# The first product of a squared-ReLU MLP as seven block products, with first and second product by turns

## The chip, the cores and the metric

The kernel runs on one core of a Trainium2 chip. The metric is device time in microseconds (us) of one execution. The kernel before the change takes 1112.21 us (median of three runs, 1112.17 to 1113.17).

Names used below: PE is the matrix engine (its weight loads have a queue of their own in the profile, PEld), DVE the vector engine, ACT the scalar engine, POOL the general-purpose engine, SP the engine that here only issues DMAs. Each engine works through its own list of instructions in the order of that list; an instruction that waits for a semaphore holds back everything behind it on the same engine. DMAs are issued from SP (plain loads), from POOL (loads that add into their destination) and, in a few places, from ACT.

## What is computed

A two-layer decoder trunk of 512 tokens with 1024 features: a gated linear attention layer, then a stick-breaking attention layer, each followed by a layer norm, an MLP and another layer norm. The change touches the MLP of both layers:

```python
def sq_relu_mlp(x, w_up, w_down):
    h = jax.nn.relu(x @ w_up)
    return (h * h) @ w_down

for layer in range(DEPTH):            # DEPTH = 2
    ...                               # mix = gla_mixer(...) or attention
    h = layer_norm(DEEPNORM_ALPHA * h + mix, ln_g[layer, 0], ln_b[layer, 0])
    h = layer_norm(DEEPNORM_ALPHA * h + sq_relu_mlp(h, mlp_w_up[layer], mlp_w_down[layer]),
                   ln_g[layer, 1], ln_b[layer, 1])
```

x is 512 x 1024, w_up 1024 x 4096, w_down 4096 x 1024, all float32.

## The kernel before

**Three products for one.** Each float32 operand is split in two reduced-precision parts, hi and lo, and a product is hi·hi + hi·lo + lo·hi: three PE instructions for each 128x128 block of the stationary operand (`mm3`, L91 to L95, or the same three written out). A weight tile of 128x1024 elements is split by `split_tile` (L66): an ACT copy makes hi (L70), a DVE subtraction makes lo (L72). hi and lo tiles come from two rings of six buffers each, raw tiles from one of three (L60). `put` (L97 to L99) does the same for activations, into tiles called T (`unit`).

**Seven for eight.** `seven` (L300) computes a product of 1024 inner elements as a 2x2 by 2x2 block product with seven block products in place of eight, at the price of sums and differences of blocks. Its moving operand is a weight block of 512 columns, its stationary operand 128 tokens of activations. Of the eight weight tiles B of a call, two blocks come as sums made by the DMA (a plain load on SP, L320, then an accumulating load on POOL onto the same tile, L314) and two more sums are made by DVE from tiles in place (L379, L389), or, with `ends`, by further accumulating loads. Each block product is 24 PE instructions of 512 columns (L355) for each of two row tiles of 128 tokens; DVE adds each result from PSUM to the residual rows h (`Rows.add`, L167 and L169).

**The MLP** (`mlp`, L694) works on groups of 512 of the 4096 inner features, eight a layer. `up(g)` computes one group of the first product directly: 8 blocks of the inner dimension x 4 blocks of features x 3 parts, 96 PE instructions with 512 tokens as moving columns (the group g = 0 in two passes of 256 tokens each, since the second half of the tokens is normalised last); then ReLU (ACT, L719) and the square (DVE L721 or ACT L723). `down(g)` is one call of `seven` on two groups. The order is up(0), up(1), up(2), down(0), up(3), up(4), down(2), and so on: between the `down` calls stand two `up` calls, which use raw tiles and no tile B.

**Around it.** `finish` (L245) follows the last product before the MLP: as row tiles of 128 tokens become complete, `stats` (a DVE reduction, two small POOL instructions L183 and L184) and `centre` (L190) normalise them, and `turn_affine` (L226) transposes them on PE, applies scale and shift on ACT (L234) and splits them into T tiles. The turns of the third and fourth row tile are handed to the MLP (`late`) and stand between the matmuls of its first group. After up(1), DVE applies the layer norm's scale and shift to the rows h themselves (`affine`, L196).

**What sets the order.** The instructions are written in program order; a scheduler then places them on the engines by readiness and priority, except those marked `keep_in_program_order`. The lists that it leaves are fixed; the chip follows them.

## Time and profile before

| | |
|---|---|
| median of the runs | 1112.21 us |
| profiled execution, its own time | 1111.48 us |
| span of the profiled execution | 1109.5 us |
| ACT busy | 571.8 us (52%) |
| POOL busy | 145.7 us (13%) |
| DMA | 169.06 MB, 152 GB/s over the span |

The span is what the profiler records between the first and the last instruction; the profiled execution's own time is 2.0 us longer. Busy time of an engine is the time in which at least one of its instructions ran. PE instructions overlap one another in the records (each is shown longer than the distance to the next), so a busy share near 100% on PE means that it never stood still for long, and its pace is read from the distance of starts.

### The profile page before, as it was taken

To read this page: it belongs to the slowest core of one execution; us is meant where nothing else is said; L and a number is where in the kernel's file an instruction comes from. 1 tells how busy PE (TensorE), PEld (TensorE's weight loads), DVE (VectorE), ACT (ScalarE), POOL (GpSimd) and SP (SyncE) were. 2 spreads that over 40 slices of the span, in tenths; PEclk is the share of its full clock that TensorE was granted. 3 is DMA by queue.
4 is the path that set the end of the run, shared out by engine and by line. 5 is a ranking of instruction groups with operands and counts; after the bars stand their busy time and mean duration, and the time that the engine had idled before them with its cause. 6 is when DMAs were issued, how large, how long until landed. Compare 5 with 4: busy or idle time off the path is not lost.

```text
span 1109.5 us, 14388 instructions
## 1 busy us (share of the span) xinstructions
PE 1100.6 (99%) x5503; PEld 912.1 (82%) x5503; DVE 817.8 (74%) x1029; ACT 571.8 (52%) x853; POOL 145.7 (13%) x177
## 2 busy tenths in 40 slices
PE   9999999999999999999999999999999999999997
PEld 7888888898888888888888777788988888888885
DVE  4687639957966856858898886688579667667677
ACT  4455437653533533536675666775635335336363
POOL 1011222210100100122202200211100000001132
PEclk9999999999999999999999999999999999999999
DMA  8441399493670670788847342443937806706774
GB/s 254 119 133 57 109 259 201 140 286 108 188 211 19 193 207 23 201 202 149 239 87 199 96 134 97 108 81 109 311 103 203 236 26 187 211 20 192 175 129 93
DMA packets 111352, 169.06 MB, mean 152 GB/s; under 512 B 13178, under 2 KB 38138, under 8 KB 111284
## 3 DMA queue, kind: packets, MB, share of 16 engines
q1 hardware_dynamic: 86228, 119.39, 32.8%
q0 software_dynamic: 22592, 44.04, 23.0%
q10 hardware_dynamic: 2464, 4.72, 1.2%
q8 instruction: 43, 0.70, 0.3%
q14 instruction: 25, 0.20, 0.1%
HBM read 162.89 MB, written 3.15 MB: 150 GB/s over the span
## 4 chain that ended last, share of the span: by engine, by line
PE 94%; DVE 3%; ACT 1%; issue 1%; POOL 0%; POOLq 0%; DVEq 0%; ACTq 0%
PE ps L355 30%; PE ps L93 18%; PE ps L94 18%; PE ps L95 18%; PE ps L796 3%; PE ps L1039 2%; PE ps L977 1%; PE ps L943 1%; PE ps L991 1%; DVE lo L72 1%; PE ps L231 1%; PE ps L584 0%; PE ps L121 0%; DVE h L167 0%; DVE c L968 0%
## 5 line engine op out<-in xcount | busy, mean ns | idle before, releaser
L355 PE MATMUL ps<-hi,T 128*128 128x512 f32 x1008 | 313.5, 390 | 0.1
L93 PE MATMUL ps<-T,hi 128*128 128x512 f32 (+1 forms) x776 | 290.4, 375 | 0.0
L94 PE MATMUL ps<-T,hi 128*128 128x512 f32 (+1 forms) x776 | 287.5, 371 | 0.5 <-DVE T L99 0.4
L95 PE MATMUL ps<-T,lo 128*128 128x512 f32 (+1 forms) x776 | 287.1, 370 | 0.0
L72 DVE TENSOR_TENSOR lo<-raw,hi 128x1024 fp32r<-128x1024 f32 x126 | 153.2, 1221 | 95.3 <-ACT hi L70 95.1
L355 PEld LDWEIGHTS ps<-hi,T 128*128 128x128 f32 x1008 | 189.0, 188 | 40.0 <-DVE T L99 0.6
L70 ACT ACTIVATE hi<-raw 128x1024 fp32r<-128x1024 f32 x128 | 135.4, 1061 | 167.4 <-PE ps L355 52.7
L70 ACT ACTIVATE hi<-B 128x1024 fp32r<-128x1024 f32 x118 | 124.4, 1059 | 173.3 <-PE ps L94 106.2
L72 DVE TENSOR_TENSOR lo<-B,hi 128x1024 fp32r<-128x1024 f32 x118 | 142.9, 1222 | 85.1 <-ACT hi L70 85.1
L355 PE MATMUL ps<-lo,T 128*128 128x512 f32 x504 | 196.3, 389 | 0.0
L95 PEld LDWEIGHTS ps<-T,lo 128*128 128x128 f32 x776 | 146.3, 189 | 24.8
L94 PEld LDWEIGHTS ps<-T,hi 128*128 128x128 f32 x776 | 146.4, 189 | 24.2 <-DVE T L99 1.0
L93 PEld LDWEIGHTS ps<-T,hi 128*128 128x128 f32 x776 | 146.1, 189 | 24.3 <-issue 1.0
L314 POOL DMA_DIRECT2D B<-in_mlp_w_down_dram x52 | 62.9, 1264 | 543.5 <-DMA B<-in_mlp_w_down_dram 342.9
L355 PEld LDWEIGHTS ps<-lo,T 128*128 128x128 f32 x504 | 94.7, 188 | 19.5
L169 DVE TENSOR_TENSOR h<-h,ps 128x512 f32<-128x512 f32 x108 | 73.4, 682 | 2.7 <-PE ps L355 2.4
L99 DVE TENSOR_TENSOR T<-s,T 128x1024 fp32r<-128x1024 f32 (+1 forms) x52 | 54.8, 1055 | 8.3 <-ACT T L98 8.3
L98 ACT ACTIVATE T<-s 128x1024 fp32r<-128x1024 f32 (+1 forms) x52 | 48.5, 937 | 21.4 <-DVE s L721 14.3
L968 DVE TENSOR_TENSOR_SCAN c<-r,c 128x384 f32<-128x384 f32 (+2 forms) x64 | 49.2, 818 | 3.3 <-ACT c L965 3.2
L93 PE MATMUL ps<-hi,T 128*128 128x512 f32 x128 | 51.4, 402 | 0.0
L719 ACT ACTIVATE s<-ps 128x512 f32<-128x512 f32 x64 | 37.8, 593 | 25.8 <-PE ps L95 25.2
L95 PE MATMUL ps<-hi,T 128*128 128x512 f32 x128 | 50.3, 393 | 0.0
(210 smaller groups left out, 1292.0 us busy)
## 6 DMA issues: line engine op xcount, KB each, us to landing
raw<-in_mlp_w_up_dram SPq DMA_DIRECT2D x64, 512.0 KB, 5.4
B<-in_mlp_w_down_dram SPq DMA_DIRECT2D x64, 512.0 KB, 5.4
B<-in_mlp_w_down_dram POOLq DMA_DIRECT2D x52, 512.0 KB, 7.8
raw<-in_gla_w_in_dram SPq DMA_DIRECT2D x20, 512.0 KB, 3.8
raw<-in_mlp_w_down_dram SPq DMA_DIRECT2D x16, 512.0 KB, 4.5
B<-in_gla_w_o_dram POOLq DMA_DIRECT2D x14, 512.0 KB, 9.0
raw<-in_kv_w_dram SPq DMA_DIRECT2D x12, 512.0 KB, 4.5
B<-in_gla_w_o_dram SPq DMA_DIRECT2D x8, 512.0 KB, 6.3
```

The costliest lines, as they stand in the source:

```text
L70: keep(nc.scalar.activation(hi, raw, AF.Copy))
L72: keep((on or nc.vector).tensor_tensor(lo, raw, hi.bitcast(F32), op=ALU.subtract))
L93: keep(nc.tensor.matmul(ps, lhsT=a[0], rhs=b[0], start=first, stop=False))
L94: keep(nc.tensor.matmul(ps, lhsT=a[0], rhs=b[1], start=False, stop=False))
L95: keep(nc.tensor.matmul(ps, lhsT=a[1], rhs=b[0], start=False, stop=last))
L98: keep(nc.scalar.activation(hi, ps, AF.Copy))
L99: keep((on or nc.vector).tensor_tensor(lo, ps, hi.bitcast(F32), op=ALU.subtract))
L169: nc.vector.tensor_tensor(h, h, ps, op=op)
L314: nc.gpsimd.dma_start(out=b.rearrange("p (a b) -> p a b", a=2), in_=weights(k, h, j), accum_op=ALU.add)
L355: nc.tensor.matmul(banks[s], lhsT=a(k, s)[x], rhs=b[k][y], start=opens and (k, x, y) == (0, 0, 0), stop=closes and (k, x, y) == (3, 1, 0), ...
L719: nc.scalar.activation(s2[:, f, :], pss[f], AF.Relu)
L968: nc.vector.tensor_tensor_scan(down, r[:, at][:, ::-1], down, 0.0, op0=ALU.mult, op1=ALU.add)
```

## The change

`up` now computes 1024 inner features a call, four calls a layer, as seven block products too. Here the weights are the stationary operand, as before (features in the rows of the result), and the moving operand is a block of 256 tokens: 7 products x 16 pairs of blocks x 3 parts = 336 PE instructions of 256 columns a call. Its seven token operands, sums and differences of blocks of x among them, are made once a layer, in the first call (c = 0), and kept (`ops`): five in T tiles, two in tiles of the hi and lo rings, which grow from six to eight buffers. Results of the block products are joined by `fresh` (ACT) and `close` (DVE additions from PSUM, then ReLU and square on ACT).

`up(c)` and `down(c)` now take turns: up(0), down(0), up(1), down(1), up(2), down(2), up(3), down(3). Both take their weight blocks from the same eight tiles B through the new class `Blocks`: (0,0) and (1,0) are loaded plainly, (0,1) and (1,1) with an accumulating load of (0,0) or (0,1) on top; `onto` then adds (1,1) onto (0,0) and (0,0) onto (1,0), by DVE or, for blocks named in `by`, by an accumulating DMA from tile to tile. The order of the loads is `AHEAD`, in up(0) its second half first. The rows' `affine` moves into up(0) and down(0). The turns of tokens 256 to 511 no longer split (class `Halves`): only x blocks (0,0) and (0,1) of tokens 0 to 255 are split at once. A few other tiles (layer-norm vectors, cumulative sums, shifted values) move into the hi and lo rings.

```diff
+            for k, j, other in order:
+                got = []
+                for h in range(2):
+                    b = pool.tile([P, 1024], F32, tag="B", bufs=8, name=nm("B"))
+                    nc.sync.dma_start(out=b.rearrange("p (a b) -> p a b", a=2), in_=weights(k, h, j))
+                    if other:
+                        nc.gpsimd.dma_start(out=b.rearrange("p (a b) -> p a b", a=2), in_=weights(other[0], h, other[1]),
+                                            accum_op=ALU.add)
...
+        def onto(self, a, b):
+            for x, y in zip(self.b[a], self.b[b]):
+                if a in self.by:
+                    nc.gpsimd.dma_start(out=x, in_=y, accum_op=ALU.add)
+                else:
+                    tt(x, x, y, op=ALU.add)
+
+    AHEAD = (0, 0, None), (1, 0, None), (0, 1, (0, 0)), (1, 1, (0, 1))
...
+        def up(c, also=()):
...
+                bs = Blocks(mlp_, w, AHEAD[2:] + AHEAD[:2], ((0, 0), (1, 0)))
...
+            product(ops[0], p1, ys, True, False, (lambda n: n == 8 and len(late) > 1 and late.pop(0)()) if c == 0 else None)
+            fresh(ys, 0, 0)
+            if c:
+                p2 = bs.pieces(1, 0)
+            product(ops[1], p2, xs, True, True, (lambda n: n == 4 and late and late.pop(0)()) if c == 0 else None)
+            close(xs, 0, 0)
+            p = bs.pieces(0, 1)
+            if c == 0:
+                r11, r21, r12, r22 = hT.r[0][:, :, LO], hT.r[0][:, :, HI], hT.r[1][:, :, LO], hT.r[1][:, :, HI]
+                t = temp()
+                tt(t, r22, r21, op=ALU.subtract)
+                ops[2] = operand(t)
+            bs.onto((0, 0), (1, 1))
+            product(ops[2], p, zs, True, False)
+            fresh(zs, 1, 1)
+            bs.onto((1, 0), (0, 0))
...
+            product(ops[3], p, ys, False, False)
+            fresh(ys, 0, 1)
...
+            product(ops[4], p, zs, False, True)
+            close(zs, 0, 1)
...
+            product(ops[5], p, ys, False, False)
+            close(ys, 1, 1)
...
+            product(ops[6], p, ys, False, True)
...
+        for c in range(NC - 1):
+            a1, a2 = up(c, turns[:2] if c == 0 else ())
+            for _ in down(c, a1, a2, by=((1, 0),), also=turns[2:] if c == 0 else ()):
                 pass
...
+        a1, a2 = up(NC - 1)
+        steps = down(NC - 1, a1, a2, norms=range(NT) if l == 0 else (2, 3), by=((0, 0), (1, 0)))
```

**The lists, at three places.** In the rows, s are the MLP's inner features, T and A split activations, B weight blocks, lo and hi their split parts, ps PSUM banks, h the residual rows; a wait on DMAHW is for a load from SP, on DMASW for a DMA from POOL.

First place: DVE at the end of an `up` and the start of the `down` behind it. Before (down(2), its first splits and the first sum of blocks among the squares of the `up` ahead):

```order
L72 TENSOR_TENSOR lo_3208<-B_3184,hi_3206 128x1024 [waits PE_49,Activation_49]
L721 TENSOR_TENSOR s_3036<-ps_2936,s_3036 128x512 [waits Activation_49]
L379 TENSOR_TENSOR B_3184<-B_3178,B_3184 128x1024 [waits DMASW2_49,DVE_49]
L721 TENSOR_TENSOR s_3036<-ps_2937,s_3036 128x512 [waits Activation_49]
L721 TENSOR_TENSOR s_3036<-ps_2938,s_3036 128x512 [waits Activation_49]
L72 TENSOR_TENSOR lo_3212<-B_3194,hi_3210 128x1024 [waits DMAHW1_49,PE_49,Activation_49]
```

Now (the end of up(2), whose fifth and sixth products are added by L830, and the first splits of down(2)):

```order
L72 TENSOR_TENSOR lo_4109<-B_4084,hi_4107 128x1024 [waits DMAHW6_49,PE_49,Activation_49]
L830 TENSOR_TENSOR s_3663<-s_3663,ps_3788 128x2x256 [waits PE_49]
L830 TENSOR_TENSOR s_3663<-s_3663,ps_3789 128x2x256 [waits PE_49]
L761 TENSOR_TENSOR B_4084<-B_4084,B_4098 128x1024 [waits DMASW4_49,DVE_49]
L72 TENSOR_TENSOR lo_4113<-B_4086,hi_4111 128x1024 [waits DMAHW7_49,Activation_49]
L761 TENSOR_TENSOR B_4086<-B_4086,B_4101 128x1024 [waits DMASW5_49,DVE_49]
L830 TENSOR_TENSOR s_3663<-s_3663,ps_3664 128x2x256 [waits PE_49]
L99 TENSOR_TENSOR T_4143<-s_3663,T_4143 128x4x256 [waits Activation_49]
L830 TENSOR_TENSOR s_3663<-s_3663,ps_3665 128x2x256 [waits PE_49]
L72 TENSOR_TENSOR lo_4148<-B_4088,hi_4146 128x1024 [waits DMAHW0_49]
```

The sum of blocks (L761) waits for the accumulating load of B_4098 and stands ahead of the second split that the first product of `down` needs (lo_4113) and ahead of the additions that close the sixth product (L830).

Second place: DVE at the end of a `down` and the start of the next `up`. Before (the last additions to the rows, then splits of raw tiles, which wait for plain loads):

```order
L167 SCALAR_TENSOR_TENSOR h_1639<-h_1639,ps_2650 128x512 [waits PE_49]
L72 TENSOR_TENSOR lo_3049<-raw_3045,hi_3047 128x1024 [waits DMAHW4_49,Activation_49]
L167 SCALAR_TENSOR_TENSOR h_1640<-h_1640,ps_2664 128x512 [waits PE_49]
L72 TENSOR_TENSOR lo_3055<-raw_3051,hi_3053 128x1024 [waits DMAHW5_49,Activation_49]
L72 TENSOR_TENSOR lo_3061<-raw_3057,hi_3059 128x1024 [waits DMAHW6_49,PE_49,Activation_49]
```

Now (the end of down(1); lo_3718 and lo_3722 are for the second product of up(2), lo_3780 and lo_3784 for its third):

```order
L72 TENSOR_TENSOR lo_3722<-B_3640,hi_3720 128x1024 [waits DMAHW7_49,Activation_49]
L761 TENSOR_TENSOR B_3634<-B_3634,B_3648 128x1024 [waits DMASW0_49,DVE_49]
L169 TENSOR_TENSOR h_1640<-h_1640,ps_3367 128x512 [waits PE_49]
L761 TENSOR_TENSOR B_3636<-B_3636,B_3651 128x1024 [waits DMASW1_49,DVE_49]
L169 TENSOR_TENSOR h_1641<-h_1641,ps_3381 128x512 [waits PE_49]
L72 TENSOR_TENSOR lo_3780<-B_3642,hi_3778 128x1024 [waits DMASW6_49,Activation_49]
```

Two sums that wait for accumulating loads have come in ahead of the splits of the third product.

Third place: POOL where the MLP of the first layer begins. Before (the statistics of the four row tiles, then accumulating loads):

```order
L184 TENSOR_TENSOR rs_1925<-ve_1924,mhalf 128x1 [waits Pool_49]
L183 TENSOR_SCALAR ve_2023<-mv_2022 128x1 [waits DVE_49]
L184 TENSOR_TENSOR rs_2024<-ve_2023,mhalf 128x1 [waits Pool_49]
L183 TENSOR_SCALAR ve_2044<-mv_2043 128x1 [waits DVE_49]
L184 TENSOR_TENSOR rs_2045<-ve_2044,mhalf 128x1 [waits Pool_49]
L314 DMA B_2614<-in_mlp_w_down_dram 128x2x512 [waits DMASW7_49,DMASW6_49,DMAHW4_49,DMASW5_49,Activation_49]
```

Now:

```order
L737 DMA B_2082<-in_mlp_w_up_dram 128x2x512 [waits DMAHW4_49,DMASW0_49]
L737 DMA B_2085<-in_mlp_w_up_dram 128x2x512 [waits DMAHW5_49]
L759 DMA B_2088<-B_2082 128x1024 [waits DMASW5_49,DMAHW6_49,DMASW0_49,Activation_49]
L759 DMA B_2090<-B_2085 128x1024 [waits DMAHW7_49,DMASW1_49]
L183 TENSOR_SCALAR ve_2020<-mv_2019 128x1 [waits DVE_49]
L184 TENSOR_TENSOR rs_2021<-ve_2020,mhalf 128x1 [waits Pool_49]
L759 DMA B_2092<-B_2088 128x1024 [waits DMAHW0_49,DMASW2_49]
L759 DMA B_2094<-B_2090 128x1024 [waits DMAHW1_49,DMASW3_49]
L183 TENSOR_SCALAR ve_2041<-mv_2040 128x1 [waits DVE_49]
L184 TENSOR_TENSOR rs_2042<-ve_2041,mhalf 128x1 [waits Pool_49]
```

The statistics of the third row tile (ve_2020) now stand behind two tile-to-tile accumulations that wait for accumulating loads, those of the fourth (ve_2041) behind two more that wait for the first two.

More of the change, by code (lines that the diff above doesn't have):

```diff
@@ L261, in finish @@
                 hs[t].centre()
-        return [lambda work, t=t: turn(t, work) for t in rest]
+        return [lambda t=t: turn(t) for t in rest]
     def rows(sp, t, pcs, ks):
@@ L741, in mlp, with temp, operand @@
-        sq.append(last)
-        steps = down(NG - 2, begun=begun, norms=range(NT) if l == 0 else (2, 3), ends=True)
-        got = done(steps, work, four, mlp_)
+            return mlp_.tile([P, 4, 512], F32, tag="s2", bufs=2, name=nm("s2"))
+        def temp():
+            return wts.tile([P, 4, 256], F32, tag="raw", bufs=3, name=nm("tmp"))
+        def operand(a, apart=False):
+            if apart:
+                us = [wts.tile([P, 2, 512], F32R, tag=tag, bufs=8, name=nm("A")) for tag in ("hi", "lo")]
+                for n, u in enumerate(us):
+                    put(u[:, :, LO], u[:, :, HI], a[:, 2 * n:2 * n + 2, :])
+            else:
+                us = [unit(F32R)]
+                put(us[0][:, :, LO], us[0][:, :, HI], a)
+            return views(us)
@@ new lines, in down, with other, add, part @@
+        def down(c, a1, a2, norms=(), by=(), also=()):
+            w = lambda k, h, j: block(mlp_w_down[l], 1024 * c + 512 * k + 256 * h, 512 * j)
+            a11, a21, a12, a22 = a1[:, :, LO], a1[:, :, HI], a2[:, :, LO], a2[:, :, HI]
+            bs = Blocks(mlp_, w, AHEAD, by)
+            ys, xs, zs = ([None, None] for _ in range(3))
+            seen = set()
+            also = list(also)
+            def other():
+                if also:
+                    also.pop(0)()
+            def add(s, banks, i, j, last=False):
+                hs[2 * i + s].add(j, banks[s], c == 0 and (i, j, s) not in seen, last and 2 * i + s in norms,
+                                  ALU.subtract if j else ALU.add)
+                seen.add((i, j, s))
+            def part(s, a, b, banks, opens, closes):
+                if opens:
+                    banks[s] = bank()
+                for k in range(4):
+                    for x, y in ((LO, 0), (LO, 1), (HI, 0)):
+                        nc.tensor.matmul(banks[s], lhsT=a(k)[:, x][:, P * s:P * s + P], rhs=b[k][y],
+                                         start=opens and (k, x, y) == (0, LO, 0),
+                                         stop=closes and (k, x) == (3, HI), skip_group_check=True)
+            def product(a, b, banks, opens, closes, i, j, last=False):
+                for s in range(2):
+                    part(s, a, b, banks, opens, closes)
+                    add(s, banks, i, j, last)
+            first = operand(a11)
+            product(first, bs.pieces(0, 0), ys, True, False, 0, 0)
+            second = operand(a12), bs.pieces(1, 0)
+            other()
+            product(*second, xs, True, True, 0, 0, last=True)
+            t = temp()
+            tt(t, a22, a21, op=ALU.subtract)
+            third = operand(t), bs.pieces(0, 1)
+            other()
+            bs.onto((0, 0), (1, 1))
+            product(*third, zs, True, False, 1, 1)
+            minus(t, t, a11)
+            bs.onto((1, 0), (0, 0))
+            fourth = operand(t), bs.pieces(0, 0)
+            product(*fourth, ys, False, False, 0, 1)
+            minus(a12, a12, t)
+            p3 = operand(a12), bs.plain(1, 1)
+            tt(a11, a11, a21, op=ALU.subtract)
+            p7 = operand(a11), bs.pieces(1, 1)
+            p4 = operand(a22), bs.pieces(1, 0)
+            for s in range(2):
+                part(s, *p3, zs, False, True)
+                add(s, zs, 0, 1, last=True)
+                yield s
+            for s in range(2):
+                part(s, *p7, ys, False, False)
+                add(s, ys, 1, 1, last=True)
+                yield ~s
+            for s in range(2):
+                part(s, *p4, ys, False, True)
+                add(s, ys, 1, 0, last=True)
+                yield 2 + s
@@ L855, in values, with done0 @@
         return held
-    def done0(steps, work, four, pool):
+    def done0(steps, four, pool):
         h2T.grow()
@@ L890, in wide @@
     def wide():
-        return [sbp.tile([P, 2 * S], F32, tag="d", bufs=2, name=nm("d")) for _ in range(2)]
+        return [wts.tile([P, 2 * S], F32, tag=tag, bufs=8, name=nm("d")) for tag in ("hi", "lo")]
     def differences(n):
```

199 lines of the change are left out of this document (134 added, 65 removed).

## The prediction

> **What bounds the kernel now.** I read the page from its head: span, busy times, slices, chain.
>
> ```profile
> span 1109.5 us, 14388 instructions
> PE 1100.6 (99%) x5503; PEld 912.1 (82%) x5503; DVE 817.8 (74%) x1029; ACT 571.8 (52%) x853; POOL 145.7 (13%) x177
> PE   9999999999999999999999999999999999999997
> DVE  4687639957966856858898886688579667667677
> PEclk9999999999999999999999999999999999999999
> DMA  8441399493670670788847342443937806706774
> PE 94%; DVE 3%; ACT 1%; issue 1%; POOL 0%; POOLq 0%; DVEq 0%; ACTq 0%
> ```
>
> PE is never idle in any slice but the last, its clock is granted in full throughout, and 94% of the chain that ended last is PE. So an instruction taken from PE is time gained, as long as the operands still come in time; and every stall of PE is time lost, since there is none now. DVE is the second engine (74%, with slices at 9), and the DMA share reaches 8 and 9 where weights are fetched. The first MLP in two stretches (an `up` with its `down`), by windows:
>
> ```profile
> core 0: us, PE busy (x) PEld busy (x) DVE busy (x) ACT busy (x) POOL busy (x), PEclk, DMA share, GB/s
> 281.80:320.00 38.20, 38.20 (x170) 31.64 (x169) 32.93 (x36) 19.48 (x20) 4.78 (x4) 1.00 0.83 224
> 320.00:363.50 43.50, 43.50 (x194) 36.03 (x193) 27.59 (x28) 15.15 (x19) 0.00 (x0) 1.00 0.23 73
> sum 81.70, PE 81.70 PEld 67.67 DVE 60.52 ACT 34.63 POOL 4.78; mean PE 40.85 PEld 33.84 DVE 30.26 ACT 17.32 POOL 2.39
> ```
>
> The first stretch is a `down`, the second two calls of `up`. PE stands at 100% in both, DVE at 86% and 63%, and DMA at 83% and 23%: the `up` calls, which need no tile B, are the time in which everything for the next `down` is fetched and summed.
>
> **The gain on PE.** The pace of PE comes from distances of starts.
>
> ```profile
> 281.97 38.08 PE ps L355 x168
> ...
> 213.40 0.28 PE L93 MATMUL ps<-T,hi 128*128 128x256 f32 x1
> ...
> 219.03 0.28 PE L95 MATMUL ps<-T,lo 128*128 128x256 f32 x1
> ```
>
> The first row, of the chain, gives 38.08/168 = 0.2267 us for 512 columns; the other two are the first and the last of 48 instructions of 256 columns (L93, L94, L95 by turns), 5.63/47 = 0.120 us. First product before, a layer: seven groups of 96 at 0.2267 and 192 half-width ones at 0.120, 152.3 + 23.0 = 175.4 us. After: 4 calls x 336 x 0.120 = 161.3 us. That is 14.1 us a layer, **28.2 us** in all. It is less than an eighth, since two of 256 columns cost 0.240 where one of 512 costs 0.227.
>
> The Trainium skill ("TensorE: Matmul & The Clock Gate", section "Wait — 56ns, not 53.3ns?") gives an instruction's time as N/2.4 GHz plus some 2.5 ns; by that, as an estimate, 512 columns take 215.8 ns and 256 take 109.2 ns, and the gain would be 38.4 us. The rows here (226.7 and 120.0) disagree.
>
> **The work added on DVE, ACT and DMA.**
>
> ```profile
> 456.97 0.68 DVE L169 TENSOR_TENSOR h<-h,ps 128x512 f32<-128x512 f32 x1
> 457.56 1.22 DVE L99 TENSOR_TENSOR T<-T,T 128x1024 fp32r<-128x1024 f32 x1
> 458.70 1.22 DVE L72 TENSOR_TENSOR lo<-raw,hi 128x1024 fp32r<-128x1024 f32 x1
> ...
> 482.79 2.00 ACT L70 ACTIVATE hi<-B 128x1024 fp32r<-128x1024 f32 x2
> ...
> L379 DVE TENSOR_TENSOR B<-B,B 128x1024 f32<-128x1024 f32 x12 | 14.6, 1216 | 0.0
> ```
>
> Behind one another, DVE starts a 512-element instruction after 0.60 us and a 1024-element one after 1.14; ACT's copies take 1.00. Seven products split 14 tiles where `up` twice split 16, but blocks used twice are split twice and the direct weights remain: 48 more splits in all (55 us), some 12 more sums of blocks (14 us), about 16 us for the operands of `up`, less 5 for squares that become fewer additions: near 80 us, DVE from 818 to about 898 us. An `up` with its `down` then asks DVE for about 63 us in 40.3 + 38.1 = 78.4 us of PE, 81% where the windows show 74%. That is no bound by itself: its cost is nothing as long as the remaining 15 us of slack a pair cover it. They don't cover a DVE that stands in front of a DMA, and that is what the lists of after show. In before, the sums of blocks never waited (L379, idle before 0.0), because the loads behind them had been out for two calls of `up`:
>
> ```profile
> 414.74 0.37 SPq L64 DMA_DIRECT2D raw<-in_mlp_w_up_dram  x1
> ...
> 441.94 12.94 SPq L320 DMA_DIRECT2D B<-in_mlp_w_down_dram  x4
> ...
> 446.03 1.20 POOL L314 DMA_DIRECT2D B<-in_mlp_w_down_dram  x1 [56.98 <-DMA B<-in_mlp_w_down_dram]
> ...
> B<-in_mlp_w_down_dram SPq DMA_DIRECT2D x64, 512.0 KB, 5.4
> B<-in_mlp_w_down_dram POOLq DMA_DIRECT2D x52, 512.0 KB, 7.8
> ...
> q1 hardware_dynamic: 86228, 119.39, 32.8%
> q0 software_dynamic: 22592, 44.04, 23.0%
> ```
>
> After, both calls use the same eight tiles B, so a load starts only when the last call has split the tile for its seventh product. SP issues one in 0.37 us. From the queues' rows a plain tile of 0.524 MB takes 0.328 x 1109.5 x 0.524/119.39 = 1.60 us of all 16 engines, an accumulated one 3.04. The page's medians from issue to landing are 5.4 and 7.8. What either takes with little beside it, and an accumulation in a crowd, by the same view over 272 to 284 us and over 388 to 396 us:
>
> ```profile
> B<-in_mlp_w_down_dram SPq DMA_DIRECT2D x1, 512.0 KB, 3.5
> B<-in_mlp_w_down_dram POOLq DMA_DIRECT2D x1, 512.0 KB, 5.9
> ...
> B<-in_mlp_w_down_dram POOLq DMA_DIRECT2D x1, 512.0 KB, 10.3
> ```
>
> I price each place with an accumulation at 5.9, 7.8 and 10.3 us, and take the middle.
>
> **From `up` to `down`** (c = 1, 2; four times). Let t be the end of the fifth product of `up`; sixth and seventh, 48 x 0.120 = 5.8 us each, end at t + 11.5. Two of eight hi buffers hold operands, so the splits of the seventh product reuse the fourth's: with ACT and DVE they are done at about t - 6.3 and t - 2.9. Then SP issues block (1,0)'s second half, (0,1) and (1,1): landings at t + 0.6 and 1.6 us apart, so B_4098's accumulation goes out at t + 5.6 and lands at t + 11.5, **13.4** or 15.9. DVE stands before L761 for it. Behind it are the sum (1.14) and lo_4113 (1.14), done at t + 15.7 in the middle case; the first product wants it at t + 13.1 (after six of its instructions): 2.6 us. B_4101 lands 1.6 us later; behind its sum stand the additions that close the sixth product, then ReLU, square and the operand a22 - a21: about 0.5 more at the second product, 2.7 at the third. Sum 4.0, **5.8**, 8.4; 23 us for four.
>
> **From `down` to `up`** (c = 2, 3; four times). With D the start of `down`, its seventh product's splits end at D + 27.0 and 28.2. SP then issues (1,0), two raw tiles, (0,1) and (1,1); the seventh of these lands at 27 + 3.5 + 6 x 1.6, so the accumulation of B_3648 goes out at D + 40.3 and lands at 46.2, 48.1 or 50.6. Two sums, two additions to the rows and the split lo_3780 end at D + 50.7, 52.7, 55.2; the third product wants it at D + 49.8: 0.9, 2.9, 5.4, and up to 4 more where the place before has made DVE late. I take **5**; 20 us for four.
>
> **Last `down` of a layer.** There `onto` for (0,0) is a tile-to-tile accumulation, which the trace doesn't show: at least nothing beyond the load before it, at most another 10.3 us. ACT's copy of the summed block stands ahead of the ReLU and square of a21 in its list. 2 to 6, **4**; twice, 8 us. The first `down` to up(1) is like the second place with earlier splits: 0 to 5, **3**; 6 us.
>
> **Where the MLP begins.** POOL's statistics now stand behind chains of accumulations.
>
> ```profile
> 216.31 0.57 POOL L184 TENSOR_TENSOR rs<-ve,mhalf 128x1 f32<-128x1 f32 x1
> ...
> 216.91 0.81 DVE L190 TENSOR_SCALAR h<-h,mv,rs 128x1024 f32<-128x1024 f32 x1 [0.65 <-POOL rs L184]
> ...
> 218.19 0.81 DVE L190 TENSOR_SCALAR h<-h,mv,rs 128x1024 f32<-128x1024 f32 x1 [0.46 <-POOL rs L184]
> ```
>
> The centring of the third and fourth row tile started 0.03 us after POOL's 0.57. Following the new list, the third's ends at 220.3 us and the fourth's, two accumulations later, starts near 227: their transposes are wanted earlier, for 4.1, **6** or 10 us in the first layer. In the second, all but the first tile's statistics may stand so: 0 to 12, **6**. Together 12.
>
> **Sum.** Stalls 23 + 20 + 8 + 6 + 12 = 69; all at their lone rows 28, all at their crowded ends 114. The profiled execution took 1111.48 us by its own time (span and 2.0 us). 1111.5 - 28.2 + 69 = 1152; I say 1150, which against the median of the runs (0.7 higher) changes nothing.
>
> **Rivals.**
> 1. *The waits are covered: faster.* If a plain load and its accumulation together take no more than about 7 us at the first place (13.1 less 2.3 of DVE leaves t + 10.8 for the landing, 5.2 us after issue), no queue stands in front of PE, and only 4 us of the starts remain: 1111.5 - 28.2 + 4 = **1087**. For it: the quickest plain load is 3.5 us. Against it: even the lone accumulation took 5.9. The Trainium skill ("DMA: Bandwidth & Descriptors", section "Anatomy of one DMA — SWDGE (gpsimd) path") gives about 2.0 us plus bytes/436e3 for such a transfer; that estimate is 3.2 us for a tile, with which this rival holds; the rows (5.9, 7.8, 10.3) disagree.
> 2. *Only the starts and the last calls pay,* the rest at lone landings: 28 us or a little less of stall, **1100 to 1112**. For it: the mean DMA rate is 152 GB/s and the windows reach 224, so a tile may land faster than the median. Against it: loads now go out in one burst, the crowded case.
> 3. *DMA or DVE is starved:* late splits make late loads, and every pair starts later than the last. All terms near their upper ends, **1175 to 1200**. For it: 81% of DVE is wanted, and SP stands in order before each tile. Against it: a stall of PE gives the others time to catch up.
>
> That the change doesn't save PE work can be left out: the count of instructions is fixed and 0.120 us was measured on the same shape.
>
> **How the numbers follow.** The forecast (1123 to 1173, centre 1150) 0.60; rival 1 0.13; rival 2 0.14, of which 0.09 faster and 0.05 the same; rival 3 0.13. Hence faster by over 0.2% 0.22, within 0.2% 0.05, slower 0.73; 0.2% is about what a measurement of this kernel can tell from no change. The range leaves out half of rival 1 and most of rival 3's upper end: 1092 to 1186.
>
> **What would show it.** Right: PE's share falls from 99% to near 93%, with idle time before the matmuls of `down` and of `up` ended by DVE's lo and T; DVE idle before L761, ended by DMA, of several us at each `up` and `down`; POOL's L183 standing behind L759; 256-column instructions of `up` 0.120 us apart. Wrong: accumulations that land within 5 us, L761 without idle time, or PE near 99% still (then rival 1). If the 256-column pitch were 0.1165 or less, a layer would cost 156.6 us or less, the gain would be 37 us or more, and the forecast would be too high by nine.

## The result, and the profile after

The changed kernel takes 1220.26 us (median of four runs, 1215.45 to 1221.53) where the kernel before takes 1112.55 in the same series: ratio 1.096, interval 1.0928 to 1.0992. The forecast was 1150 us, its range 1092 to 1186: the sign was right, the size was not. The profiled execution took 1221.53 us. One run of e1_pin_sums, below, took 2748.54 us, more than twice as long as its three others, and is left out of its median. The head of the page of after:

```profile
span 1219.8 us, 16750 instructions
PE 1113.7 (91%) x6463; PEld 963.8 (79%) x6463; DVE 895.8 (73%) x1095; ACT 672.1 (55%) x963; POOL 187.5 (15%) x217
PE   9999998599978978998899999996999979979977
PEclk9999999799998998998999899997899979989989
```

Against the page of before: PE has fallen from 99% to 91%, with slices at 5 to 8 where the MLPs lie, and in or next to the same slices the granted clock (PEclk) is no longer 9 throughout; the view of cores gives its mean as 0.949, where before it is 0.999. The busy sum of PE shows nothing of the saving (1113.7 us against 1100.6), because instructions at the lower clock last longer. So the idle time is read from the view of PE's waits in after (engine and line that wait, what for, then us in all, times, longest):

```profile
PE ps L816 <- DVE s L830: 41.6, 4, 11.0
PE ps L261 <- DVE h L190: 21.4, 5, 10.5
PE ps L909 <- ACT T L98: 15.6, 4, 6.6
PE ps L261 <- DVE mv L182: 11.5, 2, 8.1
PE ps L816 <- ACT T L98: 2.2, 2, 1.6
PE ps L816 <- DVE T L99: 2.1, 2, 1.3
```

All its rows come to 100.3 us, those of before to 3.0. So PE stands 97.3 us longer and has 28.2 us less to do: 69 us, where the span grew by 110.3. Nearly all the rest is the clock. Windows over one of the stalls (columns as in the prediction) show it:

```profile
core 0: us, PE busy (x) PEld busy (x) DVE busy (x) ACT busy (x) POOL busy (x), PEclk, DMA share, GB/s
359.00:370.00 11.00, 0.26 (x2) 0.22 (x2) 4.46 (x5) 1.01 (x1) 1.20 (x1) 0.64 0.82 153
370.00:376.00 6.00, 6.00 (x30) 6.00 (x31) 3.73 (x4) 3.02 (x3) 1.79 (x2) 0.53 0.27 53
376.00:390.00 14.00, 14.00 (x72) 11.99 (x72) 11.29 (x12) 9.43 (x12) 0.00 (x0) 1.00 0.85 238
```

PE stands for 11 us, and the granted clock falls during the stall. When PE resumes at 370, it runs the next 6 us at 0.53 and only from 376 on at full clock. In the PE timeline (start, duration, engine, line, operation) this is:

```profile
358.76 0.28 PE L816 MATMUL ps<-A,lo 128*128 128x256 f32 x1
369.78 0.80 PE L816 MATMUL ps<-T,hi 128*128 128x256 f32 x2 [10.74 <-DVE s L830]
...
375.71 0.40 PE L816 MATMUL ps<-T,hi 128*128 128x256 f32 x2
```

Between the last two rows start 27 instructions in 5.93 us; at 0.120 us each they would take 3.24. This stall costs 10.7 us of standing and 2.7 of slow running. Summed in this way over the 15 stretches of half clock in which PE had work, the slow running costs 35 to 38 us, by what is taken for the distance at full clock; PE ran for 72 us in these stretches, and half of that is 36. The whole account, place by place (stalls from the PE timeline; slow running, at its upper value, from the distances of starts in the stretch behind each; the 3.0 us of before are taken off in the row "elsewhere"):

| place | forecast | stalls | slow running behind them |
|---|---|---|---|
| `up` to `down`, four times | 23 | 41.6 | 10.1 |
| `down` to `up`, four times | 20 | 0 | 0 |
| last `down` of a layer, twice | 8 | 11.6 | 5.6 |
| first `down` of a layer | 6 | 4.0 | 3.7 |
| start of the MLP, twice | 12 | 25.0 | 10.2 |
| ahead of the first MLP, and behind it | not priced | 11.5 | 4.2 |
| elsewhere | not priced | 3.6 | 4.1 |
| sum | 69 | 97.3 | 37.9 |

Less 28.2, the two columns make 107.0 of the 110.3 us; 3.3 are not assigned (6.2 with 35 us of slow running).

**Up to down.** DVE at the end of up(1), from its timeline; the brackets hold the idle time ahead of an instruction and what ended it:

```profile
352.92 1.28 DVE L830 TENSOR_TENSOR s<-s,ps 128x512 f32<-128x512 f32 x2
365.36 1.23 DVE L761 TENSOR_TENSOR B<-B,B 128x1024 f32<-128x1024 f32 x1 [11.16 <-DMA B<-in_mlp_w_down_dram]
366.50 1.22 DVE L72 TENSOR_TENSOR lo<-B,hi 128x1024 fp32r<-128x1024 f32 x1
367.90 1.23 DVE L761 TENSOR_TENSOR B<-B,B 128x1024 f32<-128x1024 f32 x1 [0.18 <-DMA B<-in_mlp_w_down_dram]
369.04 0.68 DVE L830 TENSOR_TENSOR s<-s,ps 128x512 f32<-128x512 f32 x1
```

DVE stands 11.16 us before the sum L761 until the accumulating load has landed. Behind it stand a split, the second sum, and then the addition L830 that reads the sixth product from its PSUM bank. PE's seventh product writes to the same bank (`ys` in both calls of `product`), so PE waits for that addition, a product earlier than the forecast had it. The page's groups (busy, mean ns of one, then idle time before) and its DMA issues (median us to landing):

```profile
L761 DVE TENSOR_TENSOR B<-B,B 128x1024 f32<-128x1024 f32 x36 | 43.2, 1222 | 77.2 <-DMA B<-in_mlp_w_down_dram 44.3
...
B<-in_mlp_w_up_dram SPq DMA_DIRECT2D x64, 512.0 KB, 4.4
B<-in_mlp_w_down_dram SPq DMA_DIRECT2D x64, 512.0 KB, 4.7
B<-in_mlp_w_up_dram POOLq DMA_DIRECT2D x32, 512.0 KB, 9.3
B<-in_mlp_w_down_dram POOLq DMA_DIRECT2D x32, 512.0 KB, 9.6
B<-B POOLq DMA_DIRECT2D x28, 512.0 KB, 5.2
```

The sums, which never waited before, now wait 77.2 us in all. Plain loads got a little quicker (4.4 and 4.7 against 5.4), accumulating ones slower (9.3 and 9.6 against 7.8).

**Where the MLP begins.** From the timelines of POOL, ACT and DVE in after: the last accumulating load of the product ahead of the first MLP and the ACT copy that waits for it, then the statistics and the centring of the third row tile.

```profile
199.88 1.20 POOL L342 DMA_DIRECT2D B<-in_gla_w_o_dram  x1 [6.91 <-DMA B<-in_gla_w_o_dram]
...
207.59 1.06 ACT L70 ACTIVATE hi<-B 128x1024 fp32r<-128x1024 f32 x1 [12.44 <-DMA B<-in_gla_w_o_dram]
...
236.31 0.56 POOL L183 TENSOR_SCALAR ve<-mv 128x1 f32<-128x1 f32 x1
...
237.57 0.81 DVE L190 TENSOR_SCALAR h<-h,mv,rs 128x1024 f32<-128x1024 f32 x1 [11.78 <-POOL rs L184]
```

The lower pair was foreseen: the statistics stand behind two tile-to-tile accumulations, and DVE waits 11.78 us for them. The upper one was not: this `seven` call is not in the diff, but the scheduler has put the three chained accumulating loads of one tile behind those of the other (in before they went out by turns), and ACT waits 12.44 us for the last.

### The profile page after: what moved, and what is told of

Its sections match the earlier page's. It is cut to its first block, busy times and chain, and to the rows that moved or that the text cites. A ratio compares the mean times of both kernels' runs of the same rounds, so it can differ in the third digit from the quotient of the medians.

```text
span 1219.8 us, 16750 instructions
## 1 busy us (share of the span) xinstructions
PE 1113.7 (91%) x6463; PEld 963.8 (79%) x6463; DVE 895.8 (73%) x1095; ACT 672.1 (55%) x963; POOL 187.5 (15%) x217
## 5 line engine op out<-in xcount | busy, mean ns | idle before, releaser
L70 ACT ACTIVATE hi<-B 128x1024 fp32r<-128x1024 f32 x206 | 216.7, 1058 | 198.6 <-PE ps L909 38.9
L72 DVE TENSOR_TENSOR lo<-B,hi 128x1024 fp32r<-128x1024 f32 x206 | 247.6, 1221 | 87.8 <-ACT hi L70 87.6
L909 PE MATMUL ps<-hi,T 128*128 128x512 f32 x896 | 285.2, 398 | 15.7 <-ACT T L98 15.6
L816 PE MATMUL ps<-T,hi 128*128 128x256 f32 x1280 | 246.4, 295 | 45.8 <-DVE s L830 41.6
L816 PEld LDWEIGHTS ps<-T,hi 128*128 128x128 f32 x1280 | 211.3, 203 | 49.8 <-DVE s L830 43.4
L909 PEld LDWEIGHTS ps<-hi,T 128*128 128x128 f32 x896 | 171.4, 192 | 55.1 <-ACT T L98 17.3
L816 PE MATMUL ps<-T,lo 128*128 128x256 f32 x640 | 185.5, 293 | 0.0
L816 PEld LDWEIGHTS ps<-T,lo 128*128 128x128 f32 x640 | 129.0, 203 | 0.1
L761 DVE TENSOR_TENSOR B<-B,B 128x1024 f32<-128x1024 f32 x36 | 43.2, 1222 | 77.2 <-DMA B<-in_mlp_w_down_dram 44.3
L816 PE MATMUL ps<-A,hi 128*128 128x256 f32 x512 | 93.0, 284 | 0.8 <-ACT s L824 0.6
L816 PEld LDWEIGHTS ps<-A,hi 128*128 128x128 f32 x512 | 79.8, 192 | 1.4 <-ACT s L824 1.4
L93 PE MATMUL ps<-T,hi 128*128 128x512 f32 (+1 forms) x200 | 80.1, 401 | 0.0
L95 PE MATMUL ps<-T,lo 128*128 128x512 f32 (+1 forms) x200 | 76.6, 383 | 0.0
L94 PE MATMUL ps<-T,hi 128*128 128x512 f32 (+1 forms) x200 | 76.5, 382 | 0.0
L816 PE MATMUL ps<-A,lo 128*128 128x256 f32 x256 | 72.4, 283 | 0.0
```

The source lines that it names most:

```text
L70: keep(nc.scalar.activation(hi, raw, AF.Copy))
L72: keep((on or nc.vector).tensor_tensor(lo, raw, hi.bitcast(F32), op=ALU.subtract))
L93: keep(nc.tensor.matmul(ps, lhsT=a[0], rhs=b[0], start=first, stop=False))
L94: keep(nc.tensor.matmul(ps, lhsT=a[0], rhs=b[1], start=False, stop=False))
L95: keep(nc.tensor.matmul(ps, lhsT=a[1], rhs=b[0], start=False, stop=last))
L761: tt(x, x, y, op=ALU.add)
```

## The experiments

In each, PE's idle time is the sum of all rows of its view of waits: 100.3 us in after. The edits are to the changed kernel.

**Theory and rival for the largest place.** The theory: the sum L761, too early in DVE's list, holds up the additions, and through the PSUM bank the seventh product. The rival: PE wants the loads' blocks anyway, and if the sum stood later, PE would wait for those instead.

*e1_pin_sums.* The scheduler may no longer move `down`'s first sums ahead of what is written before them.

```diff
-        def onto(self, a, b):
+        def onto(self, a, b, keep=lambda ins: ins):
...
-                    tt(x, x, y, op=ALU.add)
+                    keep(tt(x, x, y, op=ALU.add))
...
-            bs.onto((0, 0), (1, 1))
+            bs.onto((0, 0), (1, 1), tc.keep_in_program_order)
```

The last two lines stand in `down`.

> Edit: in down, the two DVE sums of (1,1) onto (0,0) (L761) may no longer stand ahead of the splits of the third product; nothing else is pinned. Theory 1 (order): these sums, waiting for accumulating loads, held back the additions that read the sixth product's banks, which the seventh writes again. Then the four stalls before the seventh product (10.7, 11.0, 11.0, 8.8 us in the changed kernel's trace) go, and with each some 2.5 us of half clock: about 50 us less, 1170 us. Rival (the loads are late for whoever uses them): the stalls move to the fourth product of down, and no more than 15 us are gained, 1205 us or more.

Measured: 1163.54 us (median of three), ratio to before 1.0461 [1.0439, 1.0483], PE's idle time 59.7 us. The two largest rows of PE's waits in e1 were second and third in after:

```profile
PE ps L261 <- DVE h L190: 21.3, 5, 10.4
PE ps L909 <- ACT T L98: 13.7, 4, 5.9
```

The row L816 <- DVE s L830 is gone, all four stalls with it, and no other has grown by over 2 us. In e1's DVE timeline the first of these sums now starts without idle time before it, 4 us into the first product of `down` (from 367.0):

```profile
371.07 1.22 DVE L761 TENSOR_TENSOR B<-B,B 128x1024 f32<-128x1024 f32 x1
```

The gain of 56.7 us (55.1 by the spans of the profiled executions) is more than the idle time (41.6): with the slow running behind these stalls (10.1) it is 51.7, and some 4 us are not assigned. So the loads are in time, and the wait is one of order alone; the rival falls.

*e2_other_banks.* The order stays, but the seventh product gets PSUM banks of its own. It leaves out the sum of the earlier products in that quarter of the features.

```diff
-            product(ops[5], p, ys, False, False)
+            product(ops[5], p, ys, False, True)
...
-            product(ops[6], p, ys, False, True)
+            ys = [None, None]; product(ops[6], p, ys, True, True)
```

> Edit: the seventh product of up goes to two PSUM banks of its own, and the sum of the earlier products is left out of that quarter of the features; the order on DVE at the ends of the second and third up is unchanged, so the sums (L761) still stand where they stood. Theory 1a (banks): the seventh product then starts at once; DVE still stands before the sums until about t + 11.7, so what is left is what the prediction worked out for a lone landing, about 4 us at each of the four places in place of 10.4, and less half clock: 1185 to 1195 us. Rival (the seventh product waits for something else that is late at the same moment): no change, 1215 to 1221 us.

Measured: 1213.51 us, 1.0893 [1.0868, 1.0919], idle 93.4 us: a miss. Rows of PE's waits in e2:

```profile
PE ps L909 <- ACT T L98: 25.9, 8, 7.3
...
PE ps L909 <- DVE h L169: 10.0, 4, 3.4
PE ps L909 <- DVE lo L72: 9.2, 8, 2.0
```

The wait at L816 is gone as the theory says, but `down` then waits for the split behind the sum (9.2), for the additions to the rows h, which DVE reaches late (10.0), and for an operand (25.9 against 15.6). Together that is 29.5 us, 7.4 a place in place of 10.4. It bears on the forecast: even with its premise (the first waiter is `down`'s first product) the place would have cost more than the 5.8 us it gave, since it followed the two splits and left out the backlog behind them.

*e3_keep_warm.* The stalls stay, but PE runs 85 products whose results nothing reads during each of the four. It tells the clock from the idle time.

```diff
+            if c in (1, 2):
+                spare = bank()
+                for n in range(85):
+                    tc.keep_in_program_order(nc.tensor.matmul(spare[:, 0:256], lhsT=ops[5](0)[:, 0:P], rhs=ops[5](0)[:, LO],
+                                                              start=True, stop=True, skip_group_check=True))
             product(ops[6], p, ys, False, True)
```

> Edit: between the sixth and the seventh product of the second and third up, 85 matmuls of 256 columns into a spare bank, which nobody reads, 85 x 0.12 = 10.2 us at full clock, about the length of the four stalls. All other lists stay as they are. If the half clock behind each stall comes from PE standing still, no half-clock stretch is left at these four places, each gives back about 2.5 us, less up to 1.4 us where the stall was shorter: about 8 us less than the changed kernel, 1212 us. Rival (the clock falls for another reason, such as load on the chip): the half-clock stretches stay and the time is the same or longer, 1220 us or more.

Measured: 1214.87 us, 1.0946 [1.0913, 1.0980], mean clock 0.972. The windows of e3 over the same stall:

```profile
359.00:370.00 11.00, 11.00 (x94) 11.00 (x93) 2.36 (x2) 2.49 (x3) 2.31 (x2) 1.00 1.03 204
370.00:376.00 6.00, 4.68 (x37) 4.27 (x36) 5.82 (x6) 2.12 (x2) 0.66 (x1) 1.00 0.01 4
```

DVE comes to the additions no earlier (the sum waits 11.19 us in e3), yet the clock stays at 1.00 on both sides, here and at the other three places. So the half clock is a consequence of standing. The execution is 5.4 us shorter by medians (7.1 by the spans of the profiled executions), although PE did more, but the two intervals overlap: that the half clock costs time is read from the distances of starts above, not from this difference.

**Where the MLP begins.** *e4_stats_first* holds the tile-to-tile accumulations of up(0), and the last accumulating load, back until POOL's statistics have been issued (`tc.issue_after`; the list `rss` collects the last instruction of each row tile's statistics, in a line not shown).

```diff
...
+                        with tc.issue_after(rss[-3]) if order[0][2] and k and h else ExitStack():
+                            nc.gpsimd.dma_start(out=b.rearrange("p (a b) -> p a b", a=2), in_=weights(other[0], h, other[1]),
+                                                accum_op=ALU.add)
...
+                    with tc.issue_after(rss[-1]) if self.first else ExitStack():
+                        nc.gpsimd.dma_start(out=x, in_=y, accum_op=ALU.add)
```

> Edit: on POOL, in the first up of each layer, the tile-to-tile sums are issued behind the statistics of the fourth row tile, and the last accumulating load behind those of the second; order only. If POOL's queue is what held the rows' centring, the stalls of 10.5 us in the first layer and 8.1 and 2.2 us in the second go, with some 2.5 us of half clock each: 20 to 27 us less, 1193 to 1200 us. Rival (the sums themselves are then late for the fourth product): the stall moves there, and less than 8 us are gained.

Measured: 1207.80 us, 1.0867 [1.0844, 1.0890]; a gain of 12.5 where 20 to 27 were expected. The row L261 <- DVE h has shrunk from 21.4 to 1.1 us, but one product later PE has a new one (in e4 the line L816 has become L820):

```profile
PE ps L820 <- ACT T L100: 17.4, 2, 10.6
```

ACT's copy of the block that the accumulation sums stands ahead, in ACT's list, of the operand that PE wants. In the profiled execution, the quickest of four, the stall ahead of the first MLP was 3.0 us in place of 8.1, which this edit does not aim at; part of the 12.5 us may be that. *e5_act_behind* adds to e4 that this copy keeps its place behind.

```diff
-            p = bs.pieces(0, 0)
+            p = bs.pieces(0, 0, tc.keep_in_program_order) if c == 0 else bs.pieces(0, 0)
```

> Edit: the one before (statistics first on POOL), and in the first up of each layer the copies and subtractions that split the summed block (0,0) may no longer stand ahead of what is written before them on ACT and DVE. In the run before, the stalls of the first up (10.4 us in the first layer, 8.1 us in the second) came back one product later (10.6 and 6.8 us), behind an ACT copy that waited for a tile-to-tile sum. Theory (queue order on ACT): with the copies behind, both go but for the lateness of the sums themselves, 2 to 3 us in the first layer; with the half clock some 18 us less than the run before, 1188 to 1194 us. Rival (the sums are too late for the fourth product itself): the stalls move there, and less than 6 us are gained.

Measured: 1200.59 us, 1.0796 [1.0779, 1.0814]: 7.2 us less than e4, where some 18 were expected. PE's waits in e5:

```profile
PE ps L913 <- ACT T L100: 20.8, 4, 6.0
...
PE ps L820 <- ACT T L100: 7.0, 2, 6.4
```

The 10.6 us of the first layer have become 1.5; the second layer's 6.4 stay, where ACT waits for a plain load, and the stalls of the first `down` have grown from 2.1 and 1.9 to 4.9 and 4.6. Ahead of the first MLP the stall is 9.2 us, so the profiled executions of e4 and e5 differ by 6.2 us at a place that the edit does not touch. Twice, then, a wait that was taken away came back in part further down.

**The last down, and the product ahead of the MLP.** *e6_last_down* lets DVE make the sum that the last `down` made by tile-to-tile accumulation, and keeps it behind the splits of the third product; *e7_chains_by_turns* lets the two tiles of `seven` ahead of the MLP take turns in their chains of accumulating loads.

```diff
-            bs.onto((0, 0), (1, 1))
+            bs.onto((0, 0), (1, 1), tc.keep_in_program_order if c == NC - 1 else lambda ins: ins)
...
-        steps = down(NC - 1, a1, a2, norms=range(NT) if l == 0 else (2, 3), by=((0, 0), (1, 0)))
+        steps = down(NC - 1, a1, a2, norms=range(NT) if l == 0 else (2, 3), by=((1, 0),))
```

```diff
...
-        for h, (b22, b12, b11, b21) in enumerate(bs):
-            if ends:
-                for k, j in ((0, 0), (0, 1), (1, 1)):
-                    more(b21, h, k, j)
-            else:
-                tt(b21, b21, b11, op=ALU.add)
+        for k, j in ((0, 0), (0, 1), (1, 1)):
+            for h, (b22, b12, b11, b21) in enumerate(bs):
+                tc.keep_in_program_order(more(b21, h, k, j))
```

> Edit, on the changed kernel: in the last down of each layer the sum onto (0,0) is made by DVE, behind the splits of the third product, in place of a tile-to-tile accumulation. Theory (ACT's copy of the summed block stands ahead of the ReLU and square of a21 and waits for that accumulation): the stalls of 5.0 and 6.6 us go, with 2.3 and 3.3 us of half clock, 17 us less: 1200 to 1208 us. Rival (a21 is late for another reason): no change.

> Edit, on the changed kernel: in the product ahead of the first MLP, which the change does not touch, the two chains of three accumulating loads onto the halves of block (1,0) are issued by turns again, as they stood before the change; POOL's list alone differs. Theory (the new list put one chain behind the other): the stall of 8.1 us ahead of the first row tile's transposes goes, with 1.8 us of half clock: 10 us less, 1210 us. Rival (the other loads of the new first up crowd these out): no gain, 1216 us or more.

Measured: e6 1201.59 us, 1.0812 [1.0765, 1.0860], the stalls of 5.0 and 6.6 now 1.9 and 1.1; e7 1206.38 us, 1.0837 [1.0807, 1.0867], the stall of 8.1 gone. Both near what was expected: e7 gained 13.9 us for 10, and e6 gained 18.7 us, where 8.6 of stall and 5.6 of slow running make 14.2; its interval is some 10 us wide, so the difference says nothing.

**All together.** *e8_all_orders* holds the edits of e1, e4, e5, e6 and e7. It tells whether idle time and clock are the whole of the loss: the floor is then 1083 us, the time before less 28.2.

> All order edits together: sums behind the splits of the third product in every down, the last one too; statistics first on POOL; the first up's split of the summed block in written order; the chains ahead of the first MLP by turns. If the stalls are independent, 55 + 12 + 18 + 17 + 10 us are gained on 1220: 1108 us; the floor is 1111.5 less the 28.2 us that PE saves, 1083 us, and some 15 us of smaller stalls with their half clock stay: 1098 to 1112 us. Rival (DVE and the DMA queues have no room left, so a stall that goes comes back elsewhere): 1130 us or more.

Measured: 1130.02 us, 1.0165 [1.0141, 1.0189], span 1128.1, idle time 33.4 us, clock 0.989. That is a miss: 1098 to 1112 was expected, and 1130 is where the rival (stalls come back elsewhere) begins. Of the 108 us of loss 90 are gone; singly the same edits gained 109 (e1 56.7, e4 with e5 19.7, e6 18.7, e7 13.9), so they are not independent. Taking away what is left, 30.4 us of idle time above that of before and 10.4 of slow running, gives 1089: by this account, which no run shows, the saving of 28.2 us is there, within 6. The largest rows of PE's waits in e8 are of the same kind as those that went:

```profile
PE ps L910 <- ACT T L100: 10.1, 3, 4.9
PE ps L817 <- ACT T L100: 7.8, 2, 5.0
```

*e9_plain_loads_late* adds to e8 that up(0)'s plain loads are issued behind the raw tile that ACT waited for in the second layer (`rws` collects the loads of raw tiles).

```diff
...
+                    with tc.issue_after(rws[-1]) if self.first and not other else ExitStack():
+                        nc.sync.dma_start(out=b.rearrange("p (a b) -> p a b", a=2), in_=weights(k, h, j))
```

> Edit, on the run with all order edits: SP issues the four plain loads of the first up's second half behind the last raw tile of its first half; in the second layer that raw tile landed 10.0 us after its issue in a burst of eight loads, and ACT waited 5.4 us for it. SP's list alone differs, in the second layer. Theory (the burst delays the raw tile, ACT stands before it and the last turn behind that): the second layer's stall of 5.0 us before the third product goes, with 2.6 us of half clock: 1122 to 1125 us. Rival (the transfers as such fill the time, in any order): 1128 us or more.

Measured: 1126.31 us (1119.95 to 1128.27), 1.0138 [1.0123, 1.0154], a little above the 1122 to 1125 expected. In the profiled execution, the quickest of the five, the 5.0 us of the second layer have become 0.6 and 0.8. The largest that are left are 4.9 and 4.6 us in the first `down`s, where DVE also works off the rows' `affine`. Two ways of taking that from DVE, each added to e9:

```diff
-            turns = [lambda h=h: h.affine(vec, keep) for h in hs]
+            turns = [lambda h=h, on=on: h.affine(vec, keep, on) for h, on in zip(hs, (None, None, nc.gpsimd, nc.gpsimd))]
```

is *e10_affine_on_pool* (two of four row tiles on POOL), and in *e11_affine_later* two of the `affine` steps stand behind the third product of the first `down`, each ahead of its addition to the rows:

```diff
-            other()
...
-            other()
             bs.onto((0, 0), (1, 1), tc.keep_in_program_order)
-            product(*third, zs, True, False, 1, 1)
+            for s in range(2):
+                part(s, *third, zs, True, False)
+            if c:
+                for s in range(2):
+                    add(s, zs, 1, 1)
...
+            if c == 0:
+                for s in range(2):
+                    other()
+                    add(s, zs, 1, 1)
```

> Edit, on the run before: in the first down of each layer the layer norm's scale and shift of the third and fourth row tile (eight instructions of 512 elements, 4.9 us on DVE) is done by POOL, which is idle there. Theory (DVE has no room left in the first down, so the sums and the fourth operand come late): the stalls of 4.9 and 4.6 us there go, with 1.8 and 2.1 us of half clock: 1109 to 1114 us, about the kernel before. Rival (POOL's work slows DVE, or POOL is late for the additions to these rows): 1120 us or more.

> Edit, on the run with all order edits and late plain loads (1126 us): in the first down of each layer the layer norm's scale and shift of the third and fourth row tile stays on DVE, but stands, with the first additions to these rows, behind the sums and the operand of the fourth product, where nothing waits for it. Theory (in the first down DVE has no room, and this work stood ahead of what the fourth product wants): the stalls of 4.9 and 4.6 us there shrink to 2 us or less, most of 1.5 and 2.3 us of half clock goes too: 1115 to 1119 us, still above the kernel before. Rival (the fourth product waits for its sum's transfer, not for DVE): 1125 us or more.

Measured: e10 1135.22 us, 1.0213 [1.0188, 1.0238]; e11 1125.50 us, 1.0116 [1.0098, 1.0134]. Both missed. One of e10's groups on POOL, columns as in the page:

```profile
L200 POOL TENSOR_TENSOR h<-h,lng 128x512 f32<-128x512 f32 x8 | 16.2, 2038 | 0.0
```

POOL takes 2.04 us in the mean for a form of instruction that takes DVE 0.68 (and 1.40 for the eight that add the shift), and the vectors it reads lie in buffers of the hi and lo rings, so ACT's next copies waited for POOL (22.0 us over two waits). In e11 the stalls at the fourth product went, and others came at the fifth; the rows of PE's waits for that place, both layers together:

```profile
PE ps L913 <- DVE lo L76: 4.2, 2, 2.1
...
PE ps L913 <- DVE h L171: 2.8, 2, 1.4
...
PE ps L913 <- ACT T L102: 1.5, 2, 0.7
```

That is 4.2 us a layer in place of 4.9 and 4.6. The time is the one of e11's rival (1125 us or more), but not for its reason, a late transfer at the fourth product; it speaks for DVE having no room in the first `down`, wherever `affine` stands, which no run here shows by itself. No version came below the time before.

## Why the prediction was right in sign and wrong in size

**The bound: right.** PE had no idle time to lose, so every stall counted in full; the account above closes within 3 to 6 us.

**The gain on PE: right.** The rate of the new instructions is the one forecast. From the PE timeline of after, a stretch without a stall:

```profile
225.97 0.40 PE L816 MATMUL ps<-T,hi 128*128 128x256 f32 x2
...
227.65 0.28 PE L816 MATMUL ps<-T,lo 128*128 128x256 f32 x1
```

Fourteen starts in 1.68 us, 0.120 each; no gain was missing there. (A block product of `down` is 24 instructions in all, 12 for each of its two row tiles, and not 24 for each; the prediction's 168 a call are right.)

**The work on DVE: right.** 898 us forecast, 895.8 in the page. DVE was not starved by its work, but by the order in which it stood before DMAs: that e1 gains 57 us without taking one instruction from DVE shows it.

**From `up` to `down`: mechanism right, size wrong.** "DVE stands before L761 for it" holds, and the landing was near the forecast's quick end. With t at 353.25 (the stall's start, 359.04, less 5.8) the accumulation was issued at t + 3.2, where t + 5.6 was forecast, and L761 started at t + 12.1. The step that failed is "the first product wants it at t + 13.1": the first to be held up is the seventh product of `up`, at t + 5.8, through the PSUM bank that L830 reads. The additions L830 were named among what stands behind L761, but only for the operand that they lead to, not for the bank that they free. Four places: 41.6 for 23. e1 and e2 show it.

**From `down` to `up`: forecast 20, measured nothing.** The step that failed is the end of the splits that the loads wait for, "D + 27.0 and 28.2". Here the start of down(1), the loads of SP, DVE's last two splits of down(1)'s tiles, POOL's accumulation, and DVE's sum and split, each from its engine's timeline:

```profile
378.23 0.40 PE L909 MATMUL ps<-hi,T 128*128 128x512 f32 x1
...
380.65 9.65 SPq L735 DMA_DIRECT2D B<-in_mlp_w_up_dram  x3
...
398.50 7.34 SPq L735 DMA_DIRECT2D B<-in_mlp_w_up_dram  x4
...
397.25 1.22 DVE L72 TENSOR_TENSOR lo<-B,hi 128x1024 fp32r<-128x1024 f32 x1
...
400.82 1.22 DVE L72 TENSOR_TENSOR lo<-B,hi 128x1024 fp32r<-128x1024 f32 x1
...
411.69 1.20 POOL L737 DMA_DIRECT2D B<-in_mlp_w_up_dram  x1 [4.02 <-DMA B<-in_mlp_w_up_dram]
...
419.04 1.22 DVE L761 TENSOR_TENSOR B<-B,B 128x1024 f32<-128x1024 f32 x1 [5.26 <-DMA B<-in_mlp_w_up_dram]
...
424.29 2.35 DVE L72 TENSOR_TENSOR lo<-B,hi 128x1024 fp32r<-128x1024 f32 x2
```

SP issued the first four loads up to D + 12 and the last four from D + 20.3, right behind the first of the two splits, which ended at D + 20.2 and D + 23.8, some 7 and 4 us earlier than forecast. So the accumulation went out at D + 33.5 where D + 40.3 was forecast; the sum still waited (5.26 us), but lo was ready at D + 47.3, ahead of D + 49.8. The same wait in front of the same kind of instruction cost 10.7 us in one place and nothing here: what decides is what PE wants from behind it, and when.

**Start, first and last `down`: right in kind, too small.** The last `down`s cost 11.6 us for 8, where ACT's copy of the summed block holds up an operand, as forecast. The first ones cost 4.0 for 6, but within the `down`, at its fourth product, and not behind it. The starts cost 25.0 for 12: the first of the late transposes alone 10.5 and 8.1, where "4.1, 6 or 10" had the right value as its upper end.

**Not foreseen at all.** First, 11.5 us ahead of the first MLP and behind it. The 8.1 ahead of it stand where the diff changes nothing: the forecast compared the lists at three places, and not where the code had stayed the same; e7 shows it. What brought the 3.4 behind it was not followed. Second, and largest, the clock. The forecast read it as "granted in full throughout" and priced a stall at its length; the 15 slow stretches behind the stalls cost about 2.5 us each. Without these 35 to 38 us the time would have been about 1182 to 1185 us, at the upper end of the range; this is worked out, not shown, since e3 kept the clock at four of the places only.

**The rivals.** The third (all terms near their upper ends, 1175 to 1200) came nearest, though not for its reason: late splits did not make late loads. The first asked for a landing by t + 10.8 if no queue was to stand in front of PE. The sum started at t + 12.1, and e1 showed that even this would have cost nothing had the sum stood later. Two slips in the prediction's sums change nothing: the upper ends of the stalls add up to 115, not 114, and the "about 7 us" of the first rival does not fit its own 5.2 us after issue behind a plain load of at least 3.5.

## What to carry to other kernels

When an instruction that waits for a DMA comes into an in-order list, follow everything behind it on that engine, the reads of PSUM banks first: the bank that they free can stop the matrix engine sooner than the operand that the wait is for. Compare the lists of the whole program, since a scheduler also moves code that nobody changed. And price a stall of PE that was never idle at its length plus what the clock takes behind it.

## What was not expected of the hardware

**Short stalls can halve the clock.** A stall of 2.14 us at 298.1 us in after was followed by this window:

```profile
300.60:304.00 3.40, 3.40 (x10) 2.58 (x9) 3.40 (x4) 2.66 (x4) 0.00 (x0) 0.50 1.00 217
```

PE was busy throughout, at a granted clock of 0.50, and lost 1.7 us. A stall of 1.86 us that ended at 914.3 was followed by 3.41 us at half clock. Around two stalls of 0.88 and 1.06 us, which ended at 676.8 and 679.7, 6.8 us of half clock began within the second. The stretches last 3.4 us or multiples of it (3.41, 6.83, 10.24, 13.65), and in each trace they start on one grid of that step: in after at 211.86, 232.34 and 300.61 us, 6 and 20 steps apart. In e4 the same stall of 2.14 us (292.58 to 294.72) left the clock at 1.00: a slow stretch of that trace starts at 239.08, and its grid, 16 steps on, has a border at 293.69, so that no step held more than 1.1 us of the stall, where in after all of it lay between 297.19 and 300.61. So the price of a short stall hangs on where it falls; what share of a step must be idle was not measured. The Trainium skill ("TensorE: Matmul & The Clock Gate", section "Part 1: The HAM clock gate (the "warmup" mystery)") describes a free-running window of about 3.4 us, with the clock halved after an idle window and restored after a busy one. The lengths and the grid here agree; that a whole window must be idle does not, since 2.14 and 1.86 us of it were enough.

**Accumulating loads in a burst.** Their median rose from 7.8 to 9.3 and 9.6 us in the changed kernel, where each call fetches its eight plain and four accumulating loads in a group, while the median of the plain ones fell. That the grouping is the cause was not tested.
